# A two-layer decoder trunk in float32: the second weight sum of a strided pair moves from VectorE to GpSimd

## The chip, the cores and the metric

The kernel runs on one core of a Trainium2 chip. The metric is the device time of one launch in microseconds (us). TensorE multiplies matrices, ScalarE applies functions and casts, VectorE and GpSimd do elementwise work, and SyncE issues the transfers between HBM and the on-chip memory (SBUF). Each engine takes its instructions from a queue of its own, in order; semaphores tie the queues together.

## The reference

Two layers, each a mixer and a feed-forward part, then a final normalisation, on 1024 tokens of 1024 features, all in float32:

```
h = rmsnorm(x, norm1)                      # 1024 x 1024
proj = h @ w_in                            # 1024 x 5120: q, k, v of two mixers, and gates
o_a = dilated_mixture(qa, ka, va)          # 12 heads, windows with dilation 1, 4 and 16
o_b = stick_breaking_attention(qb, kb, vb) # 4 heads
gates = sigmoid(gate_pre + b_gate)
x = x + (g_a * (o_a @ w_br_a) + g_b * (o_b @ w_br_b)) @ w_o
h2 = rmsnorm(x, norm2); a, v = split(h2 @ w_up)
x = x + (gelu(causal_conv3(a)) * v) @ w_down
```

## The kernel before

**Precision.** A float32 product is made from parts: a matrix is split into `hi` (rounded by a ScalarE cast, line 129) and `lo` (the rest, by a VectorE subtraction, line 130), and three matmuls hi\*hi, hi\*lo, lo\*hi are summed in PSUM. The helper `piece` (line 880) splits one 128 x 512 block of weights in this way, into two rings of four buffers, `w_hi` and `w_lo`.

**Seven products for eight.** Large products are computed by a scheme like Strassen's: a 2 x 2 block product with seven block products in place of eight, whose operands are sums of weight blocks and sums of activation blocks. In the mixer the dilated heads' keys, queries and values and the gates are made in 14 such units per layer, 28 in all; a unit is a "strided pair" of two 128-column pieces of `w_in` (`pair`, `pair_rest`). The first of the seven products is made early, by `ahead`; the rest by `run` in `pair_rest`.

**What a unit does with its weights.** `load` brings the unit's weights into `in_a`, a tile of four 128 x 512 blocks a11, a12, a21, a22, by two DMAs of SyncE. There are two such tiles (the ring `ql`), so a unit's weights are loaded while the unit before is computed. `run` then makes four sums in place, each over one block:

- line 1011, GpSimd: a21 = a21 + a22
- line 1014, VectorE: a11 = a21 - a11, which `piece` splits into `w6`
- line 1017, GpSimd: a12 = a12 - a11
- line 1018, GpSimd: a11 = a22 - a11, once `w6` has been split

and five blocks are split by `piece`, in the order w6, w5, w7, w3, w4, which is also the order of the matmul groups (`seven`, lines 889 to 891, into the PSUM banks `i_a` and `i_c`). VectorE adds each finished group into the unit's result `u` (lines 1031 to 1057), and `put` casts and splits it (lines 1071 to 1075) or sends it out.

**What runs beside it.** While these units run, the mixer's attention is computed on the same engines, interleaved by hand in TensorE's order. In the second half of the mixer it is the far heads, 16 items per layer (`far_item`). An item makes scores `z` on TensorE (lines 584, 585), adds a bias and takes a minimum on VectorE (line 797, which frees the bank of `z`), exponentiates on ScalarE (line 798), transposes on TensorE (lines 805 to 807), splits the result into `p1h` (ScalarE, line 129) and `p1l` (VectorE, line 130), and multiplies both with the values on TensorE (lines 815, 817). TensorE takes the part with `p1h` first and then the one with `p1l`.

**Who sets the order.** TensorE's order in the mixer is the order of the program text, as the generators produce it. The orders of VectorE, ScalarE and GpSimd are set when the kernel is built, by a list scheduler that works with priorities and with its own estimate of when an operand is ready; an engine then keeps to that order, whatever the transfers do.

Of the kernel before, what the change touches and what calls it, by code (L numbers as in the profile page):

```python
# [11 lines left out]
ALU = mybir.AluOpType  # L12
# [40 lines left out]
def trunk_kernel(ctx, tc, x, norm1, w_in, b_gate, w_br, w_o, norm2, w_up, conv_w, conv_b, w_down, norm_f, out, depth=None, probe=None):  # L53
    nc = tc.nc
    act, dve, pe, pool = nc.scalar, nc.vector, nc.tensor, nc.gpsimd
# [60 lines left out]
    def bank(tag, name):  # L116
        return ps.tile([P, 512], F32, tag=tag, name=name)

    def small(name, dtype=F32):
        return sb.tile([P, 512], dtype, tag="pt", bufs=PT, name=name)  # L120
# [756 lines left out]
    def half(n, k):  # L877
        return [(H[n][0][:, 4 * k + i, :], H[n][1][:, 4 * k + i, :]) for i in range(4)]

    def piece(src):  # L880
        hi = sb.tile([P, 512], F32R, tag="wh", bufs=4, name="w_hi")
        lo = sb.tile([P, 512], F32R, tag="wl", bufs=4, name="w_lo")
        split(hi, lo, src)
        return hi, lo

    def seven(o, w, b, first, last):
        for i, (rh, rl) in enumerate(b):
            c = slice(i * P, (i + 1) * P)
            pe.matmul(o, w[0][:, c], rh, start=(first and i == 0), stop=False, skip_group_check=True)  # L889
            pe.matmul(o, w[0][:, c], rl, start=False, stop=False, skip_group_check=True)  # L890
            pe.matmul(o, w[1][:, c], rh, start=False, stop=(last and i == 3), skip_group_check=True)  # L891
            if i == 1:
                yield
# [100 lines left out]
    def pair_rest(dense, l, offs, put, view, grid, kept):  # L994
        raw = []

        def load():
            raw.append(sb.tile([P, 4, 512], F32, tag="ql", bufs=2, name="in_a"))
            for c in range(2):
                nc.sync.dma_start(  # L1000
                    raw[0][:, 2 * c : 2 * c + 2, :].rearrange("p a (k n) -> p (a k) n", n=P),
                    w_in[l][:, offs[c] : offs[c] + P].rearrange("(k p) n -> p k n", p=P),
                )

        def run():
            if not raw:
                assert dense.loads.pop(0) is load
                load()
            a11, a12, a21, a22 = (raw[0][:, i, :] for i in range(4))
            yield  # L1010
            pool.tensor_tensor(a21, a21, a22, ALU.add)
            yield
            yield
            dve.tensor_tensor(a11, a21, a11, ALU.subtract)
            w6 = piece(a11)
            yield
            pool.tensor_tensor(a12, a12, a11, ALU.subtract)
            pool.tensor_tensor(a11, a22, a11, ALU.subtract)  # L1018
            w5 = piece(a21)
            yield  # L1020
            u = sb.tile([P, T], F32, tag="wr", bufs=NRAW, name="u")
            u1, u2 = u[:, HF:T], u[:, 0:HF]
            nc.sync.dma_start(u1, kept)
            yield
            w7 = piece(a11)
            yield
            u5 = small("u5")
            pa, pc = bank("ps", "i_a"), bank("ps", "i_c")
            yield from seven(pa, w6, S[2], True, True)
            r2 = u2  # L1030
            dve.tensor_tensor(view(r2), view(u1), grid(pa), ALU.add)
            w3 = piece(a12)
            yield "turn"
            yield
            yield from seven(pc, w5, S[1], True, True)
            dve.tensor_tensor(view(u5), view(u1), grid(pc), ALU.add)
            w4 = piece(a22)
            if dense.loads:
                dense.loads.pop(0)()
            dense.last(0)  # L1040
            yield "turn"
            yield
            yield from seven(pa, w7, S[3], False, True)
            dve.tensor_tensor(view(u5), view(u5), grid(pa), ALU.add)
            put(1, 0, u5, False)
            yield "turn"
            yield
            yield from seven(pc, w3, half(0, 1), False, True)
            dve.tensor_tensor(view(r2), view(r2), grid(pc), ALU.add)
            put(0, 0, r2, False)  # L1050
            dense.last(1)
            yield "turn"
            yield
            for word in seven(pa, w4, S[4], False, True):
                yield "turn"
                yield
            dve.tensor_tensor(view(u1), view(u1), grid(pa), ALU.add)
            put(1, 1, u1, False)
            yield

        return run, load

    def pair_kq(dense, l, g, pr):
# [811 lines left out]
```

## Time and profile before

| | |
|---|---|
| runs of the kernel before | median 2755.18 us, 2748.9 to 2756.66 us (3 runs) |
| the profiled execution's own time | 2750.49 us |
| its span, first to last instruction | 2748.7 us |
| mean granted TensorE clock | 0.994 |
| TensorE busy | 97% of the span |
| VectorE, ScalarE, GpSimd busy | 76%, 48%, 25% |
| first and last sum of line 1014 in layer 1 | 278.6 and 549.2 us |
| first and last sum of line 1014 in layer 2 | 1643.8 and 1914.7 us |

The page of a profile gives busy time by engine. The list of waits gives, for a pair "engine line <- releaser", the idle time in all, how often, and the longest. In a timeline each row is one instruction: start, duration, engine, line, what it writes and reads, and in brackets the idle time of the engine before it and what ended it. A group of rows by source line gives count and durations as least, median and most.

### The profile page before, as it was taken

What the parts mean: (1) busy time and instruction counts of PE and PEld (TensorE: products, weight loads), DVE (VectorE), ACT (ScalarE), POOL (GpSimd) and SP (SyncE); (2) the same over time, 40 slices, a digit from 0 to 9 for tenths busy, and PEclk for the clock granted to TensorE, in tenths of its full rate; (3) what the DMA queues carried; (4) which work ended last, traced back from release to release, by engine and by line L of the source; (5) the groups of instructions that cost most, each with busy time, mean ns of one, the idle gap of its engine ahead of it and who ended that gap; (6) DMA issues with size and microseconds to landing.
All of it is one profiled execution on the core that took longest, in us unless ns stands there. A gap on an engine that the chain in (4) does not pass through costs nothing. (4 is left out here: it accounts for less than half of the span.)

```text
span 2748.7 us, 36983 instructions
## 1 busy us (share of the span) xinstructions
PE 2669.9 (97%) x13098; PEld 2233.4 (81%) x13098; DVE 2098.8 (76%) x3132; ACT 1330.0 (48%) x2458; POOL 699.0 (25%) x509
## 2 busy tenths in 40 slices
PE   8999999999999999999999999998999999999999
PEld 8877877788888888888888778877888888888888
DVE  5888866676689888897657888665858888988865
ACT  5666533355455545432335665333545455554225
POOL 2004122112224433321220041221222333443110
PEclk9999999999999999999999999999999999999999
DMA  4023488764334444688401234986732434446963
GB/s 151 27 85 112 127 239 218 182 204 150 88 123 151 148 157 139 218 325 318 155 31 38 84 112 145 243 215 174 241 112 79 143 139 165 156 143 244 332 251 123
DMA packets 397637, 445.72 MB, mean 162 GB/s; under 512 B 21660, under 2 KB 318988, under 8 KB 395916
## 3 DMA queue, kind: packets, MB, share of 16 engines
q1 hardware_dynamic: 397452, 443.35, 50.6%
q8 instruction: 104, 1.70, 0.3%
q14 instruction: 81, 0.66, 0.1%
HBM read 300.61 MB, written 142.67 MB: 161 GB/s over the span
## 5 line engine op out<-in xcount | busy, mean ns | idle before, releaser
L130 DVE TENSOR_TENSOR w_lo<-up_a,w_hi 128x512 fp32r<-128x512 f32 x240 | 237.8, 997 | 20.1 <-ACT w_hi L129 20.1
L129 ACT CAST w_hi<-up_a 128x512 fp32r<-128x512 f32 x240 | 149.5, 623 | 183.2 <-PE u_a L890 43.1
L1631 DVE TENSOR_TENSOR x<-x,d_ps 128x512 f32<-128x512 f32 (+1 forms) x228 | 152.4, 673 | 77.2 <-PE d_ps L1625 76.3
L1362 POOL TENSOR_TENSOR cv<-cv 128x512 f32<-128x512 f32 x88 | 132.3, 1515 | 248.7 <-DVE cv L1357 138.9
L130 DVE TENSOR_TENSOR w_lo<-w_raw,w_hi 128x512 fp32r<-128x512 f32 x176 | 131.5, 751 | 65.7 <-ACT w_hi L129 65.2
L129 ACT CAST w_hi<-w_raw 128x512 fp32r<-128x512 f32 x176 | 109.3, 622 | 122.9 <-PE o_ps L156 67.0
L129 ACT CAST w_hi<-in_a 128x512 fp32r<-128x512 f32 x140 | 86.8, 620 | 156.9 <-PE i_a L890 80.9
L130 DVE TENSOR_TENSOR g<-cv,g 128x512 fp32r<-128x512 f32 x154 | 152.6, 992 | 5.3 <-ACT g L129 2.7
L1623 PE MATMUL d_ps<-gd_in,w_hi 128*128 128x512 f32 (+1 forms) x340 | 130.2, 383 | 1.5 <-ACT w_hi L129 1.2
L1625 PE MATMUL d_ps<-gd_in,w_lo 128*128 128x512 f32 (+1 forms) x340 | 129.8, 382 | 0.0
L1624 PE MATMUL d_ps<-gd_in,w_hi 128*128 128x512 f32 (+1 forms) x340 | 129.7, 382 | 0.0
L889 PE MATMUL u_a<-hh,w_hi 128*128 128x512 f32 x320 | 124.7, 390 | 0.3 <-DVE u L1513 0.3
L890 PE MATMUL u_a<-t_lo,w_hi 128*128 128x512 f32 x320 | 124.5, 389 | 0.0
L890 PE MATMUL u_a<-hl,w_hi 128*128 128x512 f32 x320 | 124.5, 389 | 0.0
L891 PE MATMUL u_a<-t_hi,w_lo 128*128 128x512 f32 x320 | 124.5, 389 | 0.0
L889 PE MATMUL u_a<-t_hi,w_hi 128*128 128x512 f32 x320 | 124.5, 389 | 0.0
L891 PE MATMUL u_a<-hh,w_lo 128*128 128x512 f32 x320 | 124.5, 389 | 0.0
L1623 PE MATMUL d_ps<-gd_in,wd 128*128 128x512 f32 (+1 forms) x292 | 113.9, 390 | 0.0
L627 DVE TENSOR_TENSOR_SCAN stay<-stay,zero 128x128 f32<-128x128 f32 (+3 forms) x64 | 89.0, 1390 | 32.6 <-ACT stay L625 32.0
L129 ACT CAST g<-cv 128x512 fp32r<-128x512 f32 x154 | 95.0, 617 | 38.9 <-POOL cv L1362 30.0
L1018 POOL TENSOR_TENSOR in_a<-in_a 128x512 f32<-128x512 f32 x28 | 38.3, 1369 | 294.4 <-DVE w_lo L130 294.4
L1625 PE MATMUL d_ps<-gd_in,wd 128*128 128x512 f32 (+1 forms) x292 | 112.8, 386 | 0.0
(390 smaller groups left out, 8726.6 us busy)
## 6 DMA issues: line engine op xcount, KB each, us to landing
gd<-g SPq DMA_DIRECT2D x154, 512.0 KB, 3.8
gd_in<-gd SPq DMA_DIRECT2D x154, 512.0 KB, 6.2
up_a<-in_w_up_dram SPq DMA_DIRECT2D x80, 512.0 KB, 4.9
in_a<-in_w_in_dram SPq DMA_DIRECT2D x56, 512.0 KB, 6.0
w_raw<-in_w_in_dram SPq DMA_DIRECT2D x104, 256.0 KB, 3.0
t_kq<-tk SPq DMA_DIRECT2D x64, 384.0 KB, 7.4
wd_raw<-in_w_down_dram SPq DMA_DIRECT2D x22, 1024.0 KB, 12.8
gin<-gs SPq DMA_DIRECT2D x32, 512.0 KB, 4.3
```

The lines of the kernel that those rows point to most:

```text
L129: act.copy(hi, src)
L130: dve.tensor_tensor(lo, src, f32(hi), ALU.subtract)
L627: dve.tensor_tensor_scan(rev, rev, zero[:, 0:1].to_broadcast([P, L]), 1.0, ALU.mult, ALU.add)
L889: pe.matmul(o, w[0][:, c], rh, start=(first and i == 0), stop=False, skip_group_check=True)
L890: pe.matmul(o, w[0][:, c], rl, start=False, stop=False, skip_group_check=True)
L891: pe.matmul(o, w[1][:, c], rh, start=False, stop=(last and i == 3), skip_group_check=True)
L1018: pool.tensor_tensor(a11, a22, a11, ALU.subtract)
L1362: return lambda: pool.tensor_tensor(dst, a, b, ALU.subtract)
L1623: pe.matmul(o[:, sub], wh[:, c], gh[:, sub], start=(i == 0 and k in (0, 4, 5)), stop=False, skip_group_check=True)
L1624: pe.matmul(o[:, sub], wh[:, c], gl[:, sub], start=False, stop=False, skip_group_check=True)
L1625: pe.matmul(o[:, sub], wl[:, c], gh[:, sub], start=False, stop=(i == m - 1), skip_group_check=True)
L1631: dve.tensor_tensor(x, x, o[:, sub], ALU.add)
```

## The change

The sum of line 1014 is issued to GpSimd, whose queue already holds the other three. Nothing else is edited: operands, shapes and the program's order of the calls stay.

```diff
             pool.tensor_tensor(a21, a21, a22, ALU.add)
             yield
             yield
-            dve.tensor_tensor(a11, a21, a11, ALU.subtract)
+            pool.tensor_tensor(a11, a21, a11, ALU.subtract)
             w6 = piece(a11)
             yield
             pool.tensor_tensor(a12, a12, a11, ALU.subtract)
             pool.tensor_tensor(a11, a22, a11, ALU.subtract)
```

## The prediction

> **What bounds the kernel now.** I read the page first, then the list of waits, then the timeline of single stalls, engine by engine.
>
> ```profile
> span 2748.7 us, 36983 instructions
> PE 2669.9 (97%) x13098; PEld 2233.4 (81%) x13098; DVE 2098.8 (76%) x3132; ACT 1330.0 (48%) x2458; POOL 699.0 (25%) x509
> ```
>
> TensorE (PE) sets the end. It is idle for 2748.7 - 2669.9 = 79 us, so an edit on another engine gains only by shortening those idle stretches, or by keeping TensorE's clock up. The waits say what ended them, and how the four sums of a unit wait for each other.
>
> ```profile
> PE o L815 <- DVE p1l L130: 23.8, 16, 4.4
> PE z L584 <- DVE st L797: 5.0, 2, 2.8
> PE i_a L889 <- DVE u L1049: 2.3, 2, 1.3
> POOL in_a L1018 <- DVE w_lo L130: 294.4, 28, 35.8
> POOL in_a L1011 <- DMA in_a<-in_w_in_dram: 104.0, 24, 10.3
> POOL in_a L1017 <- DVE in_a L1014: 71.9, 28, 13.2
> DVE in_a L1014 <- POOL in_a L1011: 57.5, 21, 4.5
> ```
>
> Read from below, this is a chain. VectorE (DVE) stands still for 57.5 us in 21 of 28 units with L1014 at the head of its queue. It waits for GpSimd's (POOL's) L1011, and that waits 104.0 us for the weights to land. The three rows on top are TensorE waiting for VectorE's results that have nothing to do with these weights: 23.8 + 5.0 + 2.3 = 31.1 us. The timeline shows that they are one thing. At 456.9 us VectorE comes to L1014:
>
> ```profile
> 456.34 0.56 DVE L130 TENSOR_TENSOR p1l<-t,p1h 128x384 fp32r<-128x384 f32 x1 [1.40 <-ACT p1h L129]
> 461.39 0.69 DVE L1014 TENSOR_TENSOR in_a<-in_a 128x512 f32<-128x512 f32 x1 [4.49 <-POOL in_a L1011]
> 462.00 0.68 DVE L1049 TENSOR_TENSOR u<-u,i_c 128x512 f32<-128x512 f32 x1
> 462.60 1.38 DVE L130 TENSOR_TENSOR w_lo<-in_a,w_hi 128x512 fp32r<-128x512 f32 x1
> 463.89 0.54 DVE L130 TENSOR_TENSOR p1l<-t,p1h 128x384 fp32r<-128x384 f32 x1
> ```
> ```profile
> 457.98 0.48 ACT L129 CAST p1h<-t 128x384 fp32r<-128x384 f32 x1 [0.32 <-PE t L807]
> ```
> ```profile
> 460.06 1.29 POOL L1011 TENSOR_TENSOR in_a<-in_a 128x512 f32<-128x512 f32 x1 [7.03 <-DMA in_a<-in_w_in_dram]
> 462.16 1.27 POOL L1017 TENSOR_TENSOR in_a<-in_a 128x512 f32<-128x512 f32 x1 [0.80 <-DVE in_a L1014]
> ```
> ```profile
> 460.79 0.40 PE L891 MATMUL i_a<-hh,w_lo 128*128 128x512 f32 x1
> 461.02 0.28 PE L815 MATMUL o<-p1h,t_v 128*128 128x256 f32 x1
> 464.49 0.58 PE L815 MATMUL o<-p1l,t_v 128*128 128x256 f32 x1 [3.19 <-DVE p1l L130]
> 465.73 0.63 PE L890 MATMUL i_a<-t_lo,w_hi 128*128 128x512 f32 x1
> ```
>
> ScalarE (ACT) has `p1h` ready at 458.46 us, but `p1l` starts only at 463.89, behind L1014 and two operations that had waited with it. TensorE wants `p1l` at about 461.3 and idles 3.19 us. Then its matmuls take 0.63 us in place of 0.40: the clock has been halved, as the windows show.
>
> ```profile
> 463.80:470.70 6.90, 6.21 (x16) 5.05 (x17) 2.56 (x6) 1.00 (x2) 0.00 (x0) 0.51 0.54 159
> 508.20:511.60 3.40, 3.19 (x9) 2.68 (x10) 0.62 (x2) 0.00 (x0) 0.00 (x0) 0.50 0.94 202
> 1791.60:1798.40 6.80, 6.09 (x20) 5.21 (x21) 3.69 (x13) 3.31 (x9) 0.00 (x0) 0.50 1.05 240
> 1870.10:1877.00 6.90, 5.48 (x16) 4.51 (x17) 3.58 (x6) 1.10 (x2) 0.35 (x1) 0.51 0.65 168
> ```
>
> The first column of each row is the stretch, then its length, then TensorE's busy time; the granted clock is the third number from the right. Four stretches at half clock lie in the two layers' pair stages. The first follows the stall above, the others these:
>
> ```profile
> 508.41 0.58 PE L815 MATMUL o<-p1l,t_v 128*128 128x256 f32 x1 [4.40 <-DVE p1l L130]
> 1792.31 0.47 PE L584 MATMUL z<-t_kq 128*128 128x128 f32 x1 [2.76 <-DVE st L797]
> 1871.52 0.58 PE L815 MATMUL o<-p1l,t_v 128*128 128x256 f32 x1 [4.43 <-DVE p1l L130]
> ```
>
> **The change, term by term.** Taken off VectorE: 28 sums and their waits. Put on GpSimd: 28 sums. The prices:
>
> ```profile
> L1011 POOL TENSOR_TENSOR in_a<-in_a x28: 1262/1287/1816, 268.6 to 1913.4; 128x512 f32<-128x512 f32 x28
> L1014 DVE TENSOR_TENSOR in_a<-in_a x28: 683/692/694, 278.6 to 1914.7; 128x512 f32<-128x512 f32 x28
> L1017 POOL TENSOR_TENSOR in_a<-in_a x28: 1267/1294/1684, 279.3 to 1915.5; 128x512 f32<-128x512 f32 x28
> L130 DVE TENSOR_TENSOR w_lo<-in_a,w_hi x140: 673/686/1751, 315.9 to 1951.0; 128x512 fp32r<-128x512 f32 x140
> ```
>
> *Removed.* VectorE gives back 28 x 0.692 = 19.4 us of work and 57.5 us of waiting, 76.9 us together. On TensorE this returns the waits that stood behind L1014. Of the 23.8 us for `p1l`, two waits have no L1014 ahead of them, since they come after the last unit's sum (549.2 and 1914.7 us):
>
> ```profile
> 577.00 0.39 PE L815 MATMUL o<-p1l,t_v 128*128 128x256 f32 x1 [0.77 <-DVE p1l L130]
> 1942.56 0.39 PE L815 MATMUL o<-p1l,t_v 128*128 128x256 f32 x1 [0.45 <-DVE p1l L130]
> ```
>
> They stay; 23.8 - 1.2 = 22.6 us go. What is late next does not fill them: in the stall shown, `p1h` ends at 458.46, so `p1l` could end near 459.1, some 2 us before TensorE wants it. The 2.3 us behind L1049 go as well, since that addition too stood behind L1014. The 5.0 us behind L797 hardly go:
>
> ```profile
> 425.06 1.75 DVE L130 TENSOR_TENSOR w_lo<-in_a,w_hi 128x512 fp32r<-128x512 f32 x1
> 427.21 0.33 PE L584 MATMUL z<-t_kq 128*128 128x128 f32 x1 [2.21 <-DVE st L797]
> ```
>
> There the `w_lo` ahead of L797 takes 1.75 us, and a third GpSimd sum next to it will not make that shorter. I take 1.0 of the 5.0 us, with 0 and 5.0 as bounds. Waits returned: 22.6 + 2.3 + 1.0 = 25.9 us.
>
> *Clock.* Three of the four slow stretches (463.8, 508.2, 1870.1) lie behind `p1l` stalls that go. Work done at half clock takes twice as long, so half of TensorE's busy time there comes back: (6.21 + 3.19 + 5.48) / 2 = 7.4 us. The fourth, at 1791.6, lies behind an L797 stall; 6.09 / 2 = 3.0 us more if it went. For the idle time that brings this on, the stall of 3.19 us was followed by a slow stretch and the one of 2.21 us at 425 was not. "TensorE: Matmul & The Clock Gate" of the Trainium skill (section "The HAM clock gate") says the clock is halved after an idle window of about 3.4 us in a free-running frame; by that rule the longest stalls are the dear ones, and the trace agrees as far as these two go.
>
> *Added on GpSimd.* The moved sum reads what L1011 has just made, and the next in GpSimd's queue, L1017, reads what it makes. GpSimd's queue in each unit is L1011, now L1014, L1017, L1018. L1017 starts about 1.29 us after L1011 in place of 0.80 (the row at 462.16); behind it stands L1018, which waits for `w_lo` of w6 for 294.4 us anyway, so nothing is queued there that could be hurt by half a microsecond. No DMA moves, and SyncE's queue is passed by nothing. The first reader of the new block elsewhere is ScalarE's cast for w6. The tightest unit that I found:
>
> ```profile
> 407.32 0.69 DVE L1014 TENSOR_TENSOR in_a<-in_a 128x512 f32<-128x512 f32 x1 [3.58 <-POOL in_a L1011]
> 410.69 0.62 ACT L129 CAST w_hi<-in_a 128x512 fp32r<-128x512 f32 x1
> ```
>
> L1011 is done just before 407.32, so the GpSimd sum would end near 408.7, 2.0 us ahead of the cast. That cover hides the extra 0.6 us of the slower sum; without it each unit would pay the 0.6 us on ScalarE.
>
> *Added on VectorE.* GpSimd's sums slow VectorE operations that read two SBUF operands: the `w_lo` at 462.60 takes 1.38 us and ends with GpSimd's L1017 plus its own time, and the worst of 140 takes 1.751 us against a median of 0.686. Each new GpSimd sum can hold one such operation for up to 1.07 us, 28 x 1.07 = 30 us of VectorE time; the least is nothing, where no such operation is due. A gain below nothing is excluded because the removed VectorE sum's own relief is counted above. I take half, 15 us, since VectorE is busy three quarters of the time. How much of VectorE's lost time reaches TensorE I take from the stall itself: 76.9 us there made (22.6 + 2.3 + 5.0) = 29.9 us here, a share of 0.39. So 15 x 0.39 = 5.9 us, between 0 and 11.7. "SBUF — State Buffer" of the Trainium skill (section "SBUF: two separate sides") calls this an exclusive lock, held for a whole instruction; by that rule the upper end would be a full GpSimd sum each, and the trace's 1.07 us lies below that.
>
> *Sum.* 25.9 + 7.4 - 5.9 = 27.4 us. Against the profiled execution's own time, 2750.49 us, that is 2723.1. The median of the runs, 2755.18, stands 4.7 us above that execution; I set the new median the same amount higher: **2727.8 us**. Best end: 22.6 + 2.3 + 5.0 + 7.4 + 3.0 = 40.3 us, 2714.9. Worst end of the same case: 24.9 + 0 + 7.4 - 11.7 = 20.6 us, 2734.6.
>
> **The rivals.**
>
> *The wait moves into ScalarE's queue (slower).* The build's scheduler may set the w6 cast earlier in ScalarE's order, now that it counts on another engine for the sum; if it stands within 1.3 us behind L1011, ScalarE waits there as VectorE did, with the `p1h` casts behind it, and `p1l` follows `p1h`. The wait is then 57.5 + 28 x 1.294 = 93.7 us against 76.9, at the same share of 0.39 that is 36.5 us on TensorE in place of 29.9, and the 5.9 us of slowed VectorE come on top: 12.5 us slower, 2767.7. It decides from the point where the cast's cover, 2.0 us in the tightest unit, is gone. For it: the order is made blind to real landings. Against it: the cast needs a free buffer of a ring of four, which sets its place. "GPSIMD Engine Reference" of the Trainium skill (section "Engine selection") speaks against the change: elementwise sums belong on VectorE, GpSimd being about twice as slow with two inputs. The trace agrees on the price (1.294 against 0.692 us).
>
> *Half comes back only.* With TensorE earlier, other `p1l` and score waits show up behind what is removed: 24.9 / 2 + 7.4 / 2 - 5.9 = 10.2 us, 2745.0. For it: VectorE is busy 76%, and the waits of 0.77 and 0.45 us above exist without L1014.
>
> *No change.* The new VectorE order puts another early operation at the head of the queue, a `w_lo` before its cast for instance, and the stalls return under another name: 2755 us. The edit itself does what it says for the mixer's 28 units; sums of weights in the feed-forward part stay on VectorE and are in no wait above.
>
> **How the numbers follow.** About 0.3% (8.3 us) is what a measurement of this kernel can tell from no change, so faster means below 2746.9 and slower above 2763.4. Chances: the forecast 0.66, half 0.12, no change 0.09, ScalarE's queue 0.13. Faster is 0.66 + 0.12 = 0.78, same 0.09, slower 0.13. The range leaves out the last two, 0.22, about 2 in 10: from just below the best end, 2713, to just above the half case, 2748.
>
> **What would show it.** Right: no L1014 among VectorE's waits; `p1l` waits of TensorE near 1 to 3 us in place of 23.8; L1049 gone; at most one slow-clock stretch in the pair stages; L1017 no longer waiting for VectorE; some `w_lo` near 1.3 to 1.8 us more than before. Wrong: a wait of ScalarE's `w_hi` for GpSimd's L1014 of tens of us, or TensorE waiting for `p1l` or `p1h` as long as before.

## The result and the profile after

The changed kernel takes 2715.82 us (median of 4 runs, 2713.98 to 2718.55) against 2755.92 us for the kernel before (4 runs, 2748.9 to 2760.78): 40.1 us less, a ratio of 0.9857 with a 95% interval of 0.9834 to 0.9881. The two profiled executions took 2714.47 and 2750.49 us, 36.0 us apart; the accounts below are of these two.

The page of the changed kernel, its first lines:

```profile
span 2712.6 us, 37003 instructions
PE 2657.8 (98%) x13098; PEld 2227.5 (82%) x13098; DVE 2105.9 (78%) x3104; ACT 1330.4 (49%) x2458; POOL 742.1 (27%) x537
```

TensorE's idle time fell from 78.8 to 2712.6 - 2657.8 = 54.8 us, which is 24.0 us, and its busy time from 2669.9 to 2657.8, which is 12.1 us. TensorE does the same matmuls in the same order in both, so its busy time fell because they ran faster or overlapped more. GpSimd (POOL) is busy 43 us longer. VectorE (DVE) is busy 7 us longer, although it lost 28 sums; in a second profile of the changed kernel (`after_again`, below) it is 0.6 us, 2099.4 against 2098.8.

The list of waits of the changed kernel, four of TensorE's rows and those of the unit's sums, and below it the row of the kernel before for `p0l`, the `lo` part of the near heads' attention:

```profile
PE o L713 <- DVE p0l L130: 8.6, 10, 2.5
PE z L584 <- DVE st L797: 2.9, 2, 1.5
PE o L815 <- DVE p1l L130: 1.5, 3, 0.7
PE i_a L889 <- DVE u L1031: 0.4, 1, 0.4
...
POOL in_a L1018 <- DVE w_lo L130: 278.9, 28, 44.3
POOL in_a L1011 <- DMA in_a<-in_w_in_dram: 111.8, 25, 8.6
```
```profile
PE o L713 <- DVE p0l L130: 3.7, 8, 0.6
```

GpSimd waits for the weights as long as before (111.8 us against 104.0), but now nobody stands behind it. The waits of VectorE at L1014 and of GpSimd's L1017 behind it have left the list. TensorE's wait for `p1l` went from 23.8 to 1.5 us, that for L1049 from 2.3 to nothing, and that for L797 from 5.0 to 2.9. The wait for `p0l` rose from 3.7 to 8.6.

The stall that the prediction took as its example, in the timelines of the changed kernel, VectorE, ScalarE (ACT), GpSimd and TensorE in this order:

```profile
456.41 0.69 DVE L1049 TENSOR_TENSOR u<-u,i_c 128x512 f32<-128x512 f32 x1 [0.32 <-PE i_c L891]
457.02 0.69 DVE L130 TENSOR_TENSOR w_lo<-in_a,w_hi 128x512 fp32r<-128x512 f32 x1
457.69 0.56 DVE L130 TENSOR_TENSOR p1l<-t,p1h 128x384 fp32r<-128x384 f32 x1
461.02 1.53 DVE L130 TENSOR_TENSOR w_lo<-in_a,w_hi 128x512 fp32r<-128x512 f32 x1
```
```profile
457.17 0.48 ACT L129 CAST p1h<-t 128x384 fp32r<-128x384 f32 x1 [0.32 <-PE t L807]
```
```profile
459.33 1.29 POOL L1011 TENSOR_TENSOR in_a<-in_a 128x512 f32<-128x512 f32 x1 [7.09 <-DMA in_a<-in_w_in_dram]
460.71 1.29 POOL L1014 TENSOR_TENSOR in_a<-in_a 128x512 f32<-128x512 f32 x1
462.08 1.62 POOL L1017 TENSOR_TENSOR in_a<-in_a 128x512 f32<-128x512 f32 x1
```
```profile
460.22 0.28 PE L815 MATMUL o<-p1h,t_v 128*128 128x256 f32 x1
460.33 0.28 PE L815 MATMUL o<-p1l,t_v 128*128 128x256 f32 x1
```

`p1l` starts 0.04 us after its cast ends at 457.65 and is ready two microseconds before TensorE takes it, without a gap. The weights land no earlier in the unit. The price is visible as well: the `w_lo` at 461.02 takes 1.53 us beside GpSimd's L1014, and L1017 takes 1.62.

Of the four stretches at half clock in the pair stages one is left, half as long, behind the remaining L797 stall of the second layer (the row of the windows view: stretch, length, TensorE busy, and the granted clock third from the right). Elsewhere, apart from the start and the end of the span, either kernel has three such stretches of 3.4 us.

```profile
1771.50:1774.90 3.40, 3.40 (x12) 2.71 (x12) 2.02 (x7) 1.84 (x6) 0.00 (x0) 0.50 1.04 242
```

### The profile page after: what moved, and what is told of

It is laid out like the page before. It is cut to its first block, busy times and chain, and to the rows that moved or that the text cites. A ratio compares the mean times of both kernels' runs of the same rounds, so it can differ in the third digit from the quotient of the medians.

```text
span 2712.6 us, 37003 instructions
## 1 busy us (share of the span) xinstructions
PE 2657.8 (98%) x13098; PEld 2227.5 (82%) x13098; DVE 2105.9 (78%) x3104; ACT 1330.4 (49%) x2458; POOL 742.1 (27%) x537
## 5 line engine op out<-in xcount | busy, mean ns | idle before, releaser
L130 DVE TENSOR_TENSOR w_lo<-in_a,w_hi 128x512 fp32r<-128x512 f32 x140 | 116.0, 828 | 4.1 <-ACT w_hi L129 3.7
L1623 PE MATMUL d_ps<-gd_in,wd 128*128 128x512 f32 (+1 forms) x292 | 113.9, 390 | 0.0
```

What stands on the lines that cost most here:

```text
L130: dve.tensor_tensor(lo, src, f32(hi), ALU.subtract)
L1623: pe.matmul(o[:, sub], wh[:, c], gh[:, sub], start=(i == 0 and k in (0, 4, 5)), stop=False, skip_group_check=True)
```

## The experiments

My theory: the gain is the wait at the head of VectorE's in-order queue, and with it the clock. The rival: it is the 19.4 us of work that VectorE no longer does. A second question was what GpSimd's extra sums cost, and where; in the changed kernel `p0l` waits had risen from 3.7 to 8.6 us. Kernels were timed against the kernel before on the same chip; `after_again`, e1, e3 and e4 ran together on one chip, where the kernel before took 2762.0 us, and e2, e5, e6 and e7 on another, where it took 2754.7. Edits are shown against the changed kernel, e3's against the kernel before.

**The changed kernel again.** 

> The changed kernel once more, as the measure for the runs beside it. Expected at 2715.8 us, within 3 us; TensorE's waits for p1l near 1.5 us, for p0l near 8.6 us.

Measured: 2719.54 us, ratio 0.9851 (0.9832 to 0.9869). 0.7 us over the expected bound, and the kernel before is longer on this chip too; the ratios agree (0.9851 and 0.9857). `p1l` waits 1.0, `p0l` waits 8.6 us.

**The wait put back, without its work.**

```diff
+            dve.tensor_copy(sb.tile([P, 1], F32, tag="mark", name="mark"), a21[:, 0:1])
             pool.tensor_tensor(a11, a21, a11, ALU.subtract)
```

> The changed kernel, with a VectorE copy of 128x1 from a21 in L1014's place in VectorE's queue: the wait for L1011 is back, its work is not (28 copies of well under 0.2 us). Theory (the wait at the head of the queue): nearly all of the time returns, 2745 to 2756, with TensorE's p1l waits at 20 us or more and VectorE's wait at this line near 57 us. Rival (the work): 2714 to 2722.

Measured: 2761.73 us, ratio 1.0021 (1.0006 to 1.0035) to the kernel before. All of the gain is gone, and a little more. Its waits:

```profile
DVE mark L1014 <- POOL in_a L1011: 66.3, 21, 5.6
PE o L815 <- DVE p1l L130: 25.1, 13, 4.2
PE z L584 <- DVE st L797: 5.1, 2, 2.8
```

and two of its stretches at half clock, back in the pair stages:

```profile
470.80:477.60 6.80, 6.39 (x17) 5.14 (x18) 2.47 (x5) 1.18 (x2) 1.01 (x1) 0.50 0.57 160
1883.90:1890.70 6.80, 5.46 (x16) 4.48 (x17) 3.51 (x6) 1.10 (x2) 1.87 (x2) 0.50 0.69 171
```

A copy of one column (median 0.154 us) that needs L1011's result costs 1.7% of the kernel. ScalarE's, GpSimd's and TensorE's orders are those of the changed kernel, and VectorE's differs, beside the 28 copies, only in the place of a `h_sum` addition near each layer's first unit. So the wait is the cause; the work is not. Other small differences in VectorE's order between the kernel before and the changed one (`h_sum`, `p0l` and `bias` in a few places) are in this kernel too, so they are not what gained. The expected range was exceeded by 6 us: with the sums also on GpSimd, this kernel pays both prices (its `p0l` waits are 8.7 us, against 3.7 in the kernel before).

**The work put back, without the wait.**

```diff
-            w4 = piece(a22)
+            w4 = piece(a22); dve.tensor_tensor(w4[1], a22, f32(w4[0]), ALU.subtract)
```

> The changed kernel with 28 more VectorE operations of 128x512 that wait for nothing new (the w_lo of w4 is computed twice): the 19.4 us of work are back, the wait is not. Theory (the wait): 2714 to 2722, at most 0.2 us per unit of the 0.69 reach TensorE. Rival (VectorE's work counts, at the share of 0.39 or more): 7.5 us or more slower than the changed kernel, 2723 and up.

Measured: 2718.83 us, ratio 0.9849 (0.9832 to 0.9866), beside 0.9851 for the changed kernel. The 28 operations took 19.7 us of VectorE's time (0.704 us each) and nothing of the kernel's that could be measured. They stand later in the unit than L1014 did, behind the split of w4; e2 shows the same for L1014's own place: it has next to no work there, and loses the gain. Together they put the rival out.

**The sum left on VectorE, but later in its queue.** `tc.issue_after(x)` orders an instruction behind x in its engine's queue; x is the unit before's L1031. (The import of `nullcontext` is left out here.)

```diff
-            dve.tensor_tensor(a11, a21, a11, ALU.subtract)
+            with tc.issue_after(dense.mark.ins) if hasattr(dense, "mark") else nullcontext(): dve.tensor_tensor(a11, a21, a11, ALU.subtract)
...
-            dve.tensor_tensor(view(r2), view(u1), grid(pa), ALU.add)
+            dense.mark = dve.tensor_tensor(view(r2), view(u1), grid(pa), ALU.add)
```

> The kernel before, L1014 on VectorE, but ordered behind L1031 of the unit before, some 10 us later, so that L1011 should be done when it comes up. VectorE keeps its 19.4 us of sums, only the wait goes. Theory (the gain is the wait at the head of VectorE's queue): at least 30 of the 40 us come, 2713 to 2726, TensorE's p1l waits under 6 us, VectorE's L1014 wait under 15 us in place of 57.5. Rival (the gain is VectorE's freed work): no gain, 2745 to 2756.

Measured: 2712.55 us, ratio 0.9827 (0.9808 to 0.9845): all of the gain, with the sum on the engine where it was, and 7 us under the changed kernel beside it (2709.9 to 2717.13 against 2715.96 to 2721.93; the intervals of the two ratios overlap). Its waits:

```profile
POOL in_a L1017 <- DVE in_a L1014: 224.7, 28, 13.2
PE o L713 <- DVE p0l L130: 3.7, 8, 0.6
PE o L815 <- DVE p1l L130: 1.7, 2, 0.9
```

VectorE has no wait at L1014 left; GpSimd waits 224.7 us for the later sum, and ScalarE's cast for w6 waits for it twice, 6.7 us in all; neither shows in TensorE's `p1l` waits. The `p0l` waits are at the 3.7 us of the kernel before. Of the kernels that compute every sum this one has the lowest median, but e1, further below, cannot be told from it (ratio 0.9828).

**The change in layer 1 alone.**

```diff
-            pool.tensor_tensor(a11, a21, a11, ALU.subtract)
+            (dve if l else pool).tensor_tensor(a11, a21, a11, ALU.subtract)
```

> The change in layer 1 alone, layer 2 as before. Theory (stalls add up, the clock stretches belong to single stalls): a gain of 36 us x 0.4 to 0.6, 2732 to 2742, TensorE's p1l waits at 11 us, all in layer 2, with the two slow-clock stretches of layer 2's pair stage still there and those of layer 1 gone. Rival (a shared cause, such as the transfers): gain well off half, all or nothing.

Measured: 2741.7 us, ratio 0.9944 (0.9928 to 0.9959): a gain of 0.56% where the whole change gives 1.43%, 0.39 of it, at the lower edge of what was expected. In its profile TensorE's `p1l` waits are 0.9 us in layer 1 and 16.4 us in layer 2, where 11 had been expected:

```profile
PE o L815 <- DVE p1l L130: 0.9, 1, 0.9
```
```profile
PE o L815 <- DVE p1l L130: 16.4, 7, 5.1
```

(the list of waits for 250 to 600 us, and for 1600 to 1980). Layer 2 has three stretches at half clock, 17.0 us (13.7 in the kernel before). Layer 1 had been expected to have none; one of 3.4 us, from 427.2 us, lies behind its L797 stall. The stalls belong to their own units and layers; no cause common to both is needed.

**The first unit of each layer back on VectorE.**

```diff
-            pool.tensor_tensor(a11, a21, a11, ALU.subtract)
+            (dve if offs[0] == OFF_VA + 256 else pool).tensor_tensor(a11, a21, a11, ALU.subtract)
```

> The change undone in the first unit of each layer alone (2 of 28), where VectorE did not wait for L1011 and where the sum on GpSimd holds up t_lo and w_lo ahead of a p0l. Theory (GpSimd's sums hold VectorE operations with two SBUF operands, and this reaches TensorE in these two units only): TensorE's waits for p0l fall from 8.6 to about 4.9 us, 3.7 us faster than the changed kernel, 2712. Rival (holding up of VectorE is paid evenly over all 28 units, 5.9 us in all as predicted): 2 of 28 units give 0.4 us, no change against the changed kernel.

Measured: 2714.69 us, ratio 0.9828 (0.981 to 0.9847), 4.9 us under the changed kernel beside it, with `p0l` waits of 4.5 us in place of 8.6. Two of 28 units hold 4.1 of the 4.9 us by which GpSimd's sums had lengthened these waits. That the 4.9 us of time are the same ones is not shown: the intervals of the two ratios overlap, and two waits of TensorE for the copy of L983, 2.0 us, are back. VectorE's timeline of the changed kernel shows how such a wait comes about, beside GpSimd's L1014 (from 271.08, 1.61 us) and L1017 (from 272.76, 1.61 us), below it TensorE's, and last L1017 in the kernel before:

```profile
271.79 1.45 DVE L130 TENSOR_TENSOR w_lo<-w_raw,w_hi 128x512 fp32r<-128x512 f32 x1
273.16 2.97 DVE L130 TENSOR_TENSOR t_lo<-h_sum,t_hi 128x512 fp32r<-128x512 f32 x3
277.26 0.68 DVE L130 TENSOR_TENSOR p0l<-t,p0h 128x512 fp32r<-128x512 f32 x1
```
```profile
271.08 1.61 POOL L1014 TENSOR_TENSOR in_a<-in_a 128x512 f32<-128x512 f32 x1
272.76 1.61 POOL L1017 TENSOR_TENSOR in_a<-in_a 128x512 f32<-128x512 f32 x1
```
```profile
277.99 0.39 PE L713 MATMUL o<-p0l,v 128*128 128x256 f32 x1 [2.48 <-DVE p0l L130]
```
```profile
279.31 1.67 POOL L1017 TENSOR_TENSOR in_a<-in_a 128x512 f32<-128x512 f32 x1 [9.45 <-DVE in_a L1014]
```

Here VectorE has no free time: the `w_lo` and the three `t_lo` took 0.68 and 1.89 us in the kernel before, so they are 1.85 us late together, and that is the 2.48 us against 0.61 that TensorE waits. Two sums do this, not the moved one alone: in the kernel before L1017 waited 9.45 us for VectorE's L1014 and ran when this work was over.

**The sum three times on GpSimd.**

```diff
-            pool.tensor_tensor(a11, a21, a11, ALU.subtract)
+            for _ in range(3): pool.tensor_tensor(a11, a21, a11, ALU.subtract)
```

> The changed kernel with the moved sum computed three times in a row on GpSimd (an odd number gives the same block), so 56 more GpSimd sums of about 1.3 to 1.6 us in the burst behind L1011. Prediction's term (every sum holds VectorE, 5.9 us per 28 sums on TensorE): 12 us slower than the changed kernel, 2728. Theory now (it reaches TensorE in the first unit of each layer only, 1.9 us a sum there): 7 to 8 us slower, 2723. Rival (the w6 cast loses its cover of about 2 us and ScalarE's queue stalls): over 15 us slower, with waits of ScalarE's w_hi for GpSimd's L1014 of 20 us or more.

Measured: 2728.57 us, ratio 0.9902 (0.9884 to 0.992). Against the ratio of 0.9857 of the changed kernel that is 0.0045 x 2755 = 12 us, the amount of the prediction's term, but not in its place:

```profile
PE o L713 <- DVE p0l L130: 13.7, 6, 4.6
PE o L815 <- DVE p1l L130: 1.0, 2, 0.8
ACT w_hi L129 <- POOL in_a L1014: 9.9, 5, 2.7
```
```profile
281.80:285.20 3.40, 3.40 (x12) 2.74 (x11) 3.36 (x7) 0.02 (x1) 0.00 (x0) 0.50 0.48 152
336.40:339.80 3.40, 3.39 (x10) 2.71 (x11) 3.40 (x7) 2.10 (x4) 0.00 (x0) 0.50 0.20 77
1633.50:1636.90 3.40, 3.40 (x11) 2.71 (x11) 3.36 (x7) 0.00 (x0) 0.00 (x0) 0.50 0.50 154
1688.10:1691.50 3.40, 3.40 (x11) 2.60 (x10) 3.40 (x7) 2.10 (x4) 0.00 (x0) 0.50 0.20 80
```

`p0l` waits rise by 5.1 us (7 to 8 had been expected), and four new stretches at half clock, which had not, lie where the near heads' attention runs, 13.59 / 2 = 6.8 us. The stretch at 1771.5 us of the changed kernel is gone here, 3.40 / 2 = 1.7 us. Together that is 10.2 us of the 12; the rest is not assigned. ScalarE's cast for w6 lost its cover in five units, 9.9 us in all, but TensorE's `p1l` waits did not rise: the slower rival's mechanism exists, and it costs nothing at this size.

**The sum left out.** w6, w7 and the block of w3 are then made from an unsummed a11.

> The changed kernel without the sum of L1014 (w6, w7 and the block a12 are then made from an unsummed a11). What GpSimd's 28 sums still cost. Prediction's term: 5.9 us faster than the changed kernel, 2710. Theory now: 3.7 us faster, all of it in the p0l waits of the first unit of each layer, 2712. Rival (they cost nothing): 2716.

Measured: 2709.91 us, ratio 0.9829 (0.9815 to 0.9844), 0.0028 x 2755 = 8 us under the changed kernel's ratio of 0.9857; the intervals overlap. `p0l` waits are 4.7 us, L797's 1.5. From the 3.9 us less in the `p0l` waits to the 8 us of the ratio, GpSimd's 28 sums thus cost some 4 to 8 us, as a rough estimate: GpSimd's order is another here, with L1017 ahead of L1011. This kernel is no faster in ratio than e3, which computes the sum.

## Why the prediction was right, and where its sizes were off

The measured 2715.82 us lies near the forecast's best end, 2714.9, and 12.0 us under its middle: 8.6 us because the two profiles differ by 36.0 us and not by 27.4, and 3.3 us by the step from a profile to the median.

*Waits returned: right.* Predicted 25.9 us, of which 22.6 for `p1l`, 2.3 for L1049 and 1.0 for L797; the profiles show 22.3, 2.3 and 2.1, together 26.7. e2, e3 and e4 show that it is the wait and not the work that counts.

*Clock: undersized.* Predicted 7.4 us. TensorE's busy time in the pair stages' stretches at half clock was 6.21 + 3.19 + 6.09 + 5.48 = 20.97 us and is 3.40; half of the difference is 8.8 us. The term that I had left out, the stretch behind the L797 stall, was halved, while that stall went from 2.76 to 1.47 us. The other 3.3 of the 12.1 us by which TensorE's busy time fell are no matter of the clock. Compared matmul by matmul, those that ran at half clock in the pair stages of the kernel before give back 8.5 us, and those at full clock in both 3.6 us, 2.7 of it at L815. A matmul right behind a stall overlaps with none before it: with `p1l` ready, the one at 460.33 adds 0.11 us to the busy time, and behind a stall the prediction's one at 577.00 added all of its 0.39. The prediction had no term for this.

*GpSimd's hold on VectorE: near in size, by luck, and wrong in place.* Predicted 5.9 us, as 15 us of VectorE's time at a share of 0.39, spread over 28 units. The durations of VectorE's other operations add up to 19.2 us more than before (14.3 in the second profile), so the 15 was near. TensorE's waits for `p0l` rose by 8.6 - 3.7 = 4.9 us, and e1 shows that 4.1 of it lies in the first unit of each layer, where nearly all of the delay reaches TensorE; elsewhere hardly any does. The prediction also let L1017 start half a us later at most; in the first units it starts 7.7 us sooner after L1011, and is about half of the hold there. The share of 0.39 was taken from a wait, and a wait is not alike a slowdown: e4's 19.7 us of VectorE work reached TensorE at a share near nothing.

*The median: undersized.* I set the new median 4.7 us above its profiled execution, as before; it stands 1.4 above. The kernel before varies more (2748.96 to 2766.79 us over nine runs, beside 2715.96 to 2721.93 over five of the changed one). The mean granted clocks of these runs, 0.989 to 0.995 and 0.995 to 0.997, suggest that stalls meet the clock differently from run to run; that was not tested.

26.7 + 8.8 - 4.9 = 30.6 of the 36.0 us between the two profiles. Another 2.1 us are two waits of TensorE for the copy of L983 that stood right behind the `p0l` stalls and are gone. The rest is the busy time of matmuls that overlap again.

*The rivals.* That the wait moves into ScalarE's queue did not happen: the build did not move one instruction in ScalarE's order. L1014 held a ScalarE cast once, for 2.5 us, although the prediction had found 2.0 us of cover in its tightest unit: in that unit of the kernel before the cast itself had waited 3.2 us for TensorE (at 482.57 us), and without the stalls it was due sooner, while the weights were not. *Half* and *no change* did not happen either: nothing of size showed up behind the `p1l` waits, of which 1.5 us are left, and no other operation took the place at the head of VectorE's queue. "Engine selection" in the Trainium skill's "GPSIMD Engine Reference" speaks for VectorE, and e3 bears it out in part: on VectorE, ordered well, the sum is some 7 us cheaper than on GpSimd, by medians whose intervals overlap. What the change gained lay in the queue and not in the engine.

## What to carry to other kernels

In an in-order queue the price of an operation is the wait that it brings to its head, for all that stand behind it: look in the list of waits for an engine that waits on behalf of something needed much later, and compare with whom TensorE waits for. Moving such an operation to the engine that makes its operand takes the wait away, but so does ordering it later on its own engine, and that leaves the cheaper engine in use. In this kernel a GpSimd sum next to VectorE work with two SBUF operands cost TensorE time mainly where VectorE had no slack; make the exceptions there. It also pays to look at what is released sooner by the move, here L1017.

## What the runs showed of the hardware

A TensorE stall need not be long to halve its clock. In the changed kernel two stalls stood in the same place of the two layers (TensorE's timeline, the stall in brackets):

```profile
426.39 0.33 PE L584 MATMUL z<-t_kq 128*128 128x128 f32 x1 [1.46 <-DVE st L797]
1770.62 0.33 PE L584 MATMUL z<-t_kq 128*128 128x128 f32 x1 [1.47 <-DVE st L797]
```

Behind the second came 3.4 us at half clock, behind the first none. The prediction had taken 2.21 us as harmless and 3.19 as harmful; the 2.76 us stall of the kernel before had already been followed by 6.8 us at half clock.

The length of a single stall is not what decides. In each trace the clock changes only on a grid of steps of 3.41 us, and what tells is TensorE's idle time within one step. In the ten traces together, without the start and the end of each, 40 steps at full clock have more than 1.80 us of idle time, and each of them was followed by half clock. 7724 have less than 1.45 us, and none was. Of the 49 between, 17 were. (The ends of matmuls are modelled, so these bounds are estimates.) In the windows view, first three steps of the kernel before, the two that share its 2.21 us stall and the one that holds most of the 3.19 us stall, then the two of the changed kernel that hold the stalls above:

```profile
422.87:426.28 3.41, 2.12 (x14) 1.72 (x12) 2.43 (x3) 0.62 (x1) 2.59 (x2) 1.00 1.05 332
426.28:429.70 3.42, 2.49 (x14) 2.18 (x15) 3.24 (x11) 2.03 (x7) 0.00 (x0) 1.00 1.02 268
460.42:463.83 3.41, 0.88 (x5) 0.47 (x3) 2.44 (x3) 0.62 (x1) 2.20 (x2) 1.00 0.15 54
```
```profile
423.19:426.60 3.41, 1.95 (x14) 1.63 (x12) 3.23 (x5) 0.86 (x2) 3.25 (x3) 1.00 1.12 350
1768.05:1771.46 3.41, 1.94 (x15) 1.62 (x14) 3.10 (x7) 1.47 (x4) 3.21 (x2) 1.00 1.09 327
```

The steps of the 2.21 us stall have 1.29 and 0.93 us of idle time each, that of the 3.19 us stall 2.53. The two of the changed kernel have 1.46 and 1.47, and lie at the edge. "TensorE: Matmul & The Clock Gate" of the Trainium skill (section "The HAM clock gate") has the clock halved after an idle window of about 3.4 us in a free-running frame. The traces agree with the frame and its length, but here a step with somewhat under half of it idle could be enough.

VectorE and GpSimd slow each other in both directions: the moved sum has a median of 1.608 us in the changed kernel and 1.286 in e2, and the `w_lo` beside it at 461.02 takes 1.53 us where their median is 0.69.
